# Sixteen 32-byte reads, one for each DMA engine, issued from the Activation queue ahead of the first load of a row-maximum kernel

## The chip, the cores and the metric

One core of a Trainium2 chip. The metric is device time in microseconds (us), median of several executions. A profile's span runs from the first to the last instruction and is about 1.8 us shorter than the device time of the same execution (165.17 and 163.4 us for the profiled run of the kernel before).

## The reference

```python
x = np.random.randn(32, 512, 1024).astype(np.float32)     # 16,384 rows of 4,096 B
return np.max(x, axis=-1).astype(np.float32)
```

## The kernel before

The rows are read in loads of decreasing size into a ring of 45 row slots per partition. Each load has one reduction on VectorE. All loads are issued by SyncE; the two stores at the end are issued by Activation. The first load gives each of 128 partitions 14 rows, which lie in one run of 14 x 4,096 = 57,344 B in memory.

```python
BLOCKS = [
    [14, 13, 12, 11, 9, 8, 8, 7, 6, 5, 5, 4, 4, 3, 3],
    [2, 2, 2, 1, 1, 1, 1, 1, 1, 1, 1, 1],
]
RING = 45
...
    PAD = 16
    tail = once.tile([P, PAD + H], F32)        # columns 0 to 7 are read by nobody
    at = first = 0
    for loads in BLOCKS:
        S = sum(loads) + (loads is BLOCKS[-1])
        xb = xf[first * P:(first + S) * P, :].rearrange("(p i) d -> p i d", p=P)
        ...
        for n in loads:
            if at + n > RING:
                at = 0
            xc = ring[:, at:at + n, :]
            nc.sync.dma_start(out=xc, in_=xb[:, b:b + n, :])
            reduce = nc.vector.reduce_max(out=res[:, first + b:first + b + n], in_=xc, axis=X)
            ...
    ...                                        # last row in two halves, then two stores
```

## Time and profile before

| | kernel before |
|---|---|
| device time | 164.99 us, median of 3 (164.94 to 165.01) |
| DMA queue of the loads | 96.6% of 16 engines' span |
| VectorE | busy 139.0 us, waits for loads 22.1 us, of it 20.31 us for the first |
| first issue, first packet, first reduction | 0.73, 1.72, 20.31 us |

What bounds the kernel, and why an earlier start of the loads should move the end by as much, is worked out in the prediction below. Its words, as this text uses them: an issue is the DMA instruction on the queue of SyncE or Activation; a packet is one record of what one of the 16 DMA engines moved; a load or read has landed when all of its data are there and what waits for it may start. A descriptor is the order for one such piece of work, and the descriptor generator makes the descriptors from an issue. Where an experiment speaks of a queue's ring, the queue's list of descriptors is meant and not the tile `ring`.

A window line can be read for more than its rate. A packet counts, with its whole length, in the stretch in which it starts. So GB/s times the stretch's length, over 57,344 B, is a number of packets; and DMA share times length times 16 is the sum of their durations. For 1.60 to 1.80 us of the kernel before: 1720 GB/s x 0.2 us / 57,344 B = 6 packets, and 5.78 x 0.2 x 16 = 18.5 us, or 3.08 us each. A steady packet takes 2.116 us. What a first packet takes beyond that is called its excess from here on.

### The profile page before, as it was taken

How to read it: one execution, taken by the hardware profiler on the slowest of the kernel's cores; microseconds unless marked ns; L12 is line 12 of the kernel's file. 1: busy time of each engine (PE TensorE's matmuls, PEld its weight loads, DVE VectorE, ACT ScalarE, POOL GpSimd, SP SyncE). 2: the span in 40 equal slices, each digit the busy share in tenths (PEclk: the TensorE clock that was granted, in tenths of full speed). 3: DMA queues.
4: the chain of work that ended last, by engine and by line, in shares of the span. 5: the costliest groups of instructions: out<-in, count | busy, mean ns of one | idle time of the engine just before them, and what ended most of it. 6: DMA issues, size and time to landing. Idle time of an engine off the chain costs nothing.

```text
span 163.4 us, 117 instructions
## 1 busy us (share of the span) xinstructions
DVE 139.0 (85%) x29; POOL 0.2 (0%) x4
## 2 busy tenths in 40 slices
DVE  0000099989998999999999999999999999999994
POOL 0000000000000000000000000000000000000000
DMA  6999999999989989999989999999999999999990
GB/s 225 449 449 449 433 417 417 417 401 529 433 385 430 452 386 432 433 433 441 457 385 481 401 442 422 409 438 421 446 409 425 437 410 422 427 407 409 409 355 16
DMA packets 4464, 67.18 MB, mean 411 GB/s; under 512 B 752, under 2 KB 752, under 8 KB 2160
## 3 DMA queue, kind: packets, MB, share of 16 engines
q1 hardware_dynamic: 4176, 67.11, 96.6%
q10 hardware_dynamic: 288, 0.07, 0.2%
HBM read 67.11 MB, written 0.07 MB: 411 GB/s over the span
## 4 chain that ended last, share of the span: by engine, by line
DVE 49%; DMA 48%; SPq 1%; issue 0%
DMA ring<-in_x_dram 48%; DVE res L58 48%; SPq L57 1%; DVE res L70 0%; DVE tail L69 0%
## 5 line engine op out<-in xcount | busy, mean ns | idle before, releaser
L58 DVE TENSOR_REDUCE res<-ring 128x1 f32<-128x1024 f32 (+12 forms) x27 | 137.7, 5165 | 22.1 <-DMA ring<-in_x_dram 22.1
L70 DVE TENSOR_REDUCE res<-tail 128x1 f32<-128x513 f32 x1 | 0.7, 686 | 0.0
L69 DVE TENSOR_REDUCE tail<-ring 128x1 f32<-128x512 f32 x1 | 0.7, 682 | 0.0
L90 POOL MEMSET const-bfloat16-1.0<- 128x1 bf16 x1 | 0.1, 102 | 0.0
L90 POOL MEMSET const-uint8-127<- 128x1 uint8 x1 | 0.1, 102 | 0.0
L90 POOL MEMSET const-float32-0.0<- 128x1 f32 x1 | 0.1, 99 | 0.2 <-issue 0.2
L90 POOL MEMSET const-float32-1.0<- 128x1 f32 x1 | 0.1, 99 | 0.0
## 6 DMA issues: line engine op xcount, KB each, us to landing
ring<-in_x_dram SPq DMA_DIRECT2D x2, 4096.0 KB, 25.6
ring<-in_x_dram SPq DMA_DIRECT2D x1, 7168.0 KB, 19.6
ring<-in_x_dram SPq DMA_DIRECT2D x1, 6656.0 KB, 34.9
ring<-in_x_dram SPq DMA_DIRECT2D x1, 6144.0 KB, 48.9
ring<-in_x_dram SPq DMA_DIRECT2D x1, 5632.0 KB, 28.5
ring<-in_x_dram SPq DMA_DIRECT2D x2, 2560.0 KB, 38.4
ring<-in_x_dram SPq DMA_DIRECT2D x1, 4608.0 KB, 24.7
ring<-in_x_dram SPq DMA_DIRECT2D x9, 512.0 KB, 13.8
```

The source lines that it names most:

```text
L57: nc.sync.dma_start(out=xc, in_=xb[:, b:b + n, :])
L58: reduce = nc.vector.reduce_max(out=res[:, first + b:first + b + n], in_=xc, axis=X)
L69: nc.vector.reduce_max(out=tail[:, PAD - 1:PAD], in_=half, axis=X)
L70: nc.vector.reduce_max(out=res[:, I - 1:], in_=tail[:, PAD - 1:], axis=X)
L90: nc = _bacc.Bacc("TRN2", target_bir_lowering=False, num_devices=1)
```

## The change

The intent: touch every DMA engine with a tiny read before the first load, so that whatever an engine's first transfer pays is paid by the tiny read. The Activation queue is used so that SyncE's own issue is not held up.

```diff
     PAD = 16
     tail = once.tile([P, PAD + H], F32)
+
+
+    far = xf.rearrange("(q i) d -> q (i d)", q=16)
+    nc.scalar.dma_start(out=tail[:16, :PAD // 2], in_=far[:, :PAD // 2])
 
     at = first = 0
```

## The prediction

> **What bounds the kernel now.** I read four views in this order: the page, the waits, the chain of work that ended last, and then narrow stretches around the first load. The page has only two workers: VectorE (DVE) and the DMA queue that SyncE feeds.
>
> ```profile
> span 163.4 us, 117 instructions
> DVE 139.0 (85%) x29; POOL 0.2 (0%) x4
> q1 hardware_dynamic: 4176, 67.11, 96.6%
> q10 hardware_dynamic: 288, 0.07, 0.2%
> L58 DVE TENSOR_REDUCE res<-ring 128x1 f32<-128x1024 f32 (+12 forms) x27 | 137.7, 5165 | 22.1 <-DMA ring<-in_x_dram 22.1
> ```
>
> The reader is to see that both workers are nearly full. The loads keep 16 DMA engines at 96.6% of the span. DVE is busy 139.0 us and idle 22.1 us, and all of that idle time is a wait for a load. Where the waits lie decides what a change is worth:
>
> ```profile
> 0.73 94.15 SPq L57 DMA_DIRECT2D ring<-in_x_dram  x14
> 20.31 15.09 DVE L58 TENSOR_REDUCE res<-ring 128x14 f32<-128x14336 f32 x1 [20.31 <-DMA ring<-in_x_dram]
> 36.05 14.02 DVE L58 TENSOR_REDUCE res<-ring 128x13 f32<-128x13312 f32 x1 [0.65 <-DMA ring<-in_x_dram]
> 50.58 12.95 DVE L58 TENSOR_REDUCE res<-ring 128x12 f32<-128x12288 f32 x1 [0.51 <-DMA ring<-in_x_dram]
> 63.91 30.14 DVE L58 TENSOR_REDUCE res<-ring 128x11 f32<-128x11264 f32 x3 [0.38 <-DMA ring<-in_x_dram]
> 94.27 8.69 DVE L58 TENSOR_REDUCE res<-ring 128x8 f32<-128x8192 f32 x1 [0.21 <-DMA ring<-in_x_dram]
> ```
>
> Five waits. The last ends at 94.27 us, where the seventh load lands; after it DVE runs to the end without a gap. So the end is the landing of load 7 plus fixed DVE work, and load 7 is one of a row of loads that run back to back from the first byte. **If the first load moves by d and the rate stays, the end moves by d**: loads 1 to 3 are issued at once, and the later ones are released by landings or reductions that move too. So the start matters one for one. There the windows show this (columns: stretch, its length, DVE and GpSimd busy, clock, DMA share, GB/s; a packet counts in the stretch in which it starts):
>
> ```profile
> 1.60:1.80 0.20, 0.00 (x0) 0.00 (x0) 1.00 5.78 1720
> 1.80:2.00 0.20, 0.00 (x0) 0.00 (x0) 1.00 3.68 1147
> 2.00:2.20 0.20, 0.00 (x0) 0.00 (x0) 1.00 1.74 573
> ...
> 2.40:2.60 0.20, 0.00 (x0) 0.00 (x0) 1.00 2.15 860
> 2.60:2.80 0.20, 0.00 (x0) 0.00 (x0) 1.00 0.68 287
> 2.80:4.50 1.70, 0.00 (x0) 0.00 (x0) 1.00 0.00 0
> 4.50:4.70 0.20, 0.00 (x0) 0.00 (x0) 1.00 3.31 1434
> 4.70:4.90 0.20, 0.00 (x0) 0.00 (x0) 1.00 4.63 2007
> 4.90:5.10 0.20, 0.00 (x0) 0.00 (x0) 1.00 1.98 860
> 5.10:5.30 0.20, 0.00 (x0) 0.00 (x0) 1.00 0.66 287
> ```
>
> A packet of the first load is one row of 14 x 4096 = 57,344 B, so 1720 GB/s over 0.2 us is 6 packets, 1147 is 4, and so on: 6 + 4 + 2 + 3 + 1 = 16 first packets, one for each engine, starting between 1.7 and 2.7 us. The second packets (5 + 7 + 3 + 1 = 16) start between 4.5 and 5.3 us. The trace's packet records, read one by one, make it exact: the first packet starts at 1.72 us, second packets start from 4.54 to 5.15 us, and every later packet of this load takes 2.116 us, which is 27.1 GB/s an engine. First packets take up to 3.38 us: **12 of the 16 are 0.5 to 1.26 us longer than a steady one**, and the four shortest (0.00 to 0.06 us over for three of them) are among those that started last. This start-up excess is what the change aims at.
>
> **What the Trainium skill says.** (1) "DMA: Bandwidth & Descriptors", section "Latency and other measured facts": about 600 ns to the first byte on this path, and about 800 ns for the smallest read of HBM. The trace has 0.99 us from the start of the first issue (0.73 us) to the first packet's start (1.72 us), so longer than the page's first figure if the start of a packet stands for its first byte. (2) The same page, "Issuing engines are not separate DMA queues": DMAs of all issuing engines run on the same 16 DMA engines and interleave. So the added reads do reach the engines that the first load uses. (3) The same page, "Why a DMA increments its semaphore by 16 and not by 1": the outer dimension sets how many engines a copy takes; 16 rows give 16, one row each. That fits the change's intent; the kernel before has no copy of this shape to check it with. (4) "Perfetto Trace Analysis", "DMA Instruction — HWDGE (DVE, Sync)": the descriptor generator is locked for one issuer at a time. The trace before has no two issuers at once, so it can't say. No page says anything of a cost of an engine's first use.
>
> **The change, part by part.** It removes nothing. It adds one DMA instruction on the Activation queue, 16 rows of 32 B from places 4 MiB apart, into bytes of the tail tile that nobody reads.
> - Bytes: 512 B against 67.11 MB, nothing.
> - Activation's time: its two stores take 0.38 and 0.34 us to issue, from 159.78 us on. Before that it idles, so a similar third issue at about 0.73 us is free there.
> - Waits: comparing the order of instructions, the eight completion semaphores that DMAs take in turn shift by one place. The only new wait is that the eighth load waits for the 16 small reads, which land some 80 us before it can be issued. Each reduction waits for the same load as before. The last load writes other columns of the tail tile and gets no wait for the reads.
> - Gain: the lead over the first load is small. In the trace SyncE and Activation leave the start barrier 0.005 us apart, so both issue at about 0.73 us. Their race is decided by who generates descriptors faster, 16 against 128 rows. If the cold part is an engine's first access, the reads take it over, but only by as much as they come sooner. I put that lead at 0 to 0.5 us. The ceiling is the slowest engine: its second packet starts at 5.15 us where 1.72 + 2.116 = 3.84 us would be ideal, so 1.3 us.
> - Cost: if the generator is held by Activation when SyncE wants it, the first load starts later by up to one issue, 0.35 us.
> - Sum: a mean gain of about 0.35 us (a quarter of the ceiling) less a mean cost of about 0.15 us (half an issue, taken less than surely), so 0.2 us: 164.99 - 0.2 = 164.8 us.
>
> **The rivals.** *Full gain:* the excess is wholly a first access that a 32 B read can take over, and the reads get there first; the whole row of loads moves by up to 1.3 us, so 163.7 us. For it speaks that steady packets vary by only a few ns, so the excess belongs to the start; against it, that the reads start no earlier than the load, and that the last-starting engines show hardly any excess, as if the delay were one common to all and over at about 2.4 to 2.7 us whatever asked first. *Hidden anyway, or cold elsewhere:* the excess belongs to SyncE's own ring or to the pages that it reads (the added reads touch other addresses), so nothing changes: 165.0 us. *A new wait in its place:* the two issuers queue for the generator and the first load starts late by 0.1 to 0.35 us, and the slowest engine's packets with it: 165.1 to 165.35 us. *DVE as the bound:* it is already the bound from load 7 to the end (94.27 us onward), but this caps nothing, because an earlier start moves load 7 too. At most 22.1 us of waits could ever be taken out and this change reaches only a fraction of the first, 20.31 us.
>
> **Range and chances.** The full gain gives 163.7, the full cost 165.35. I don't give the extremes much weight: 164.2 to 165.25 us should hold it 8 times in 10, with 164.8 us as the prediction. Repeats of the kernel before lie within 164.94 to 165.01 us, so noise adds little. Two per cent would be 3.3 us, more than twice the ceiling of the gain and nine times the cost worked out above. So same has 0.98, faster 0.01, slower 0.01.
>
> **What would show it right or wrong.** In the changed kernel's trace: (a) the packets of the Activation queue should start at or before the first load's; if they come after, the gain is nil. (b) SyncE's first issue should start at 0.73 us and last 0.37 us; a longer or later one is the generator's queue. (c) The 16 second packets should start about 0.2 us earlier at the slowest engine (5.15 us before), and the first reduction at about 20.1 us instead of 20.31. (d) The end should move by the same amount as the first reduction, within 0.1 us, with DVE's busy time at 139.0 us and the wait at load 7 still there. If the first reduction moves and the end doesn't, my chain is wrong, and a later load or the store carries the end. If the end moves more than 1.3 us, the rate of the loads changed, which I hold unlikely since 512 B can't do it.

## The result, and the profile after

The changed kernel took 164.98 us in the median (164.94 to 165.13, 4 runs), the kernel before 164.97 us beside it (164.88 to 165.01, 4 runs). The ratio is 1.0003, with a 95% interval from 0.9986 to 1.0021: the same. Ratios here are the mean time of one kernel's runs over that of the other's of the same rounds, so not quite the ratio of the medians.

The timeline of the changed kernel, with the lines that answer to those of before (start, length, engine, line, operation; L61 and L62 are the old L57 and L58):

```profile
0.72 0.40 ACTq L47 DMA_DIRECT2D tail<-in_x_dram  x1
0.73 94.09 SPq L61 DMA_DIRECT2D ring<-in_x_dram  x14
20.25 15.09 DVE L62 TENSOR_REDUCE res<-ring 128x14 f32<-128x14336 f32 x1 [20.25 <-DMA ring<-in_x_dram]
...
94.19 8.69 DVE L62 TENSOR_REDUCE res<-ring 128x8 f32<-128x8192 f32 x1 [0.21 <-DMA ring<-in_x_dram]
```

Activation issues its reads at the same moment as SyncE its first load (0.725 and 0.730 us). The first reduction starts at 20.25 us instead of 20.31. That 0.06 us must not be credited to the change: this profile is of an execution of 165.00 us, the one of before of an execution of 165.17 us, the slowest of all of that kernel's runs beside it, and the timed runs show no difference. Their interval is wide, though: it reaches from 0.23 us faster to 0.35 us slower, so the times alone can't tell the predicted gain of 0.2 us from none. What the reads did has to be read from the trace.

The windows of the changed kernel over its first packets, and over the second ones:

```profile
1.60:1.80 0.20, 0.00 (x0) 0.00 (x0) 1.00 6.32 2007
1.80:2.00 0.20, 0.00 (x0) 0.00 (x0) 1.00 6.23 2007
2.00:2.20 0.20, 0.00 (x0) 0.00 (x0) 1.00 0.89 287
2.20:2.40 0.20, 0.00 (x0) 0.00 (x0) 1.00 0.88 287
...
4.50:4.70 0.20, 0.00 (x0) 0.00 (x0) 1.00 3.32 1434
4.70:4.90 0.20, 0.00 (x0) 0.00 (x0) 1.00 5.31 2295
4.90:5.10 0.20, 0.00 (x0) 0.00 (x0) 1.00 1.33 574
```

In the first 0.2 us there are 7 packets with 6.32 x 0.2 x 16 / 7 = 2.89 us each: the excess is still there. By the packet records its median is 0.75 us, against 0.76 us before. The other thing to see is what the first four lines lack. A small read would add a packet whose bytes are too few to show; the packet records have none on the Activation queue in this time. Where the reads went is told by the DMA view (size of the issue, then microseconds to landing):

```profile
q10 hardware_dynamic: 320, 0.07, 0.2%
...
tail<-in_x_dram ACTq DMA_DIRECT2D x1, 0.5 KB, 6.8
```

Queue 10 is Activation's; it has 32 packets more than the 288 of before: 16 reads of 32 B and 16 completion writes of 4 B. They took 6.8 us to land. The packet records show why. **On each of the 16 engines the 57,344 B packet came first, and the read stands just behind it**: on the quickest engine, for example, the first packet runs from 1.730 to 4.338 us, the read from 4.335 for 9 ns, the second packet of the load from 4.340 us. The read's completion write waited for that second packet in turn and came at 6.45 us. The Trainium skill, "DMA: Bandwidth & Descriptors", section "Queues, rings and completion order", says that an engine takes turns between queues one whole packet at a time; the trace agrees, with packets of 57,344 B and a wait of 2.6 us.

So the reads warmed nothing, because they ran second. That leaves the more important question: would they have helped, had they run first?

### The profile page after: what moved, and what is told of

It reads as the page before. It is cut to its first block, busy times and chain, and to the rows that moved or that the text cites. A ratio compares the mean times of both kernels' runs of the same rounds, so it can differ in the third digit from the quotient of the medians.

```text
span 163.2 us, 118 instructions
## 1 busy us (share of the span) xinstructions
DVE 138.9 (85%) x29; POOL 0.2 (0%) x4
## 4 chain that ended last, share of the span: by engine, by line
DVE 49%; DMA 48%; SPq 1%; issue 0%
DMA ring<-in_x_dram 48%; DVE res L62 48%; SPq L61 1%; DVE res L74 0%; DVE tail L73 0%
## 5 line engine op out<-in xcount | busy, mean ns | idle before, releaser
L62 DVE TENSOR_REDUCE res<-ring 128x1 f32<-128x1024 f32 (+12 forms) x27 | 137.7, 5162 | 22.0 <-DMA ring<-in_x_dram 22.0
```

## The experiments

Theory A: the excess is a cold first access that a small read can take over, and the change failed only because its reads came late. Theory B: the excess belongs to the opening of a load, whatever went before. Eleven kernels were run. All outputs are right.

**Reads landed before the first load (e1).** The loads wait for the reads (`far` as in the change):

```diff
...
+    warm = nc.scalar.dma_start(out=tail[:16, :PAD // 2], in_=far[:, :PAD // 2])
...
+            load = nc.sync.dma_start(out=xc, in_=xb[:, b:b + n, :])
+            tc.add_manual_dep(load.ins, warm.ins.name, SYNC, reason="the start")
```

> The first load now waits until the 16 small reads have landed, so the reads really come first. Theory A (cold first access that a small read takes over; the change failed only because its reads came behind the first packets): the excess of the first 57,344 B packets over 2.116 us falls from a median of 0.75 us to under 0.1 us; the first load is issued about 2 us later, so the time is about 164.97 + 2.0 - 0.7 = 166.3 us. Theory B (the excess is the ordinary time from a descriptor's start to flowing data, paid by whatever transfer opens an empty queue): the excess stays at 0.6 to 0.9 us and the time is 164.97 plus the whole delay, about 167.0 us.

The DMA view of this run, then its windows over the first packets of the load:

```profile
tail<-in_x_dram ACTq DMA_DIRECT2D x1, 0.5 KB, 2.0
```

```profile
3.60:3.80 0.20, 0.00 (x0) 0.00 (x0) 1.00 6.21 2007
3.80:4.00 0.20, 0.00 (x0) 0.00 (x0) 1.00 4.48 1434
```

Now the reads land in 2.0 us, and the load's first issue starts at 2.71 us. But 6.21 x 0.2 x 16 / 7 = 2.84 us a packet, as before: the excess is 0.68 us in the median, 0.42 us at least. The time was 166.81 us in its one run (state unknown), 1.88 us over the 164.93 us of before in that session, for an issue 1.98 us later (2.71 against 0.73). Theory A expected 166.3, B 167.0; the excess decides for B.

This run also shows how close the race of the change was. Alone, the reads start one after another, 0.047 us apart, from 1.72 to 2.42 us; the first packets of the load in the changed kernel start from 1.72 to 2.29 us. What lets the load win on every engine stays open; e4 below, which issues both in the same way, has the same order on all 16.

**Delay without reads (e2), and a shorter delay, timed (e8).** The control for e1: the loads wait for two VectorE instructions.

```diff
+    idle = once.tile([P, 1024], F32)           # e8: 512
+    nc.vector.memset(idle, 0.0)
+    warm = nc.vector.reduce_max(out=tail[:, 1:2], in_=idle, axis=X)
...
+            tc.add_manual_dep(load.ins, warm.ins.name, SYNC, reason="the start")
```

> Control: no reads, but the first load waits for two VectorE instructions of about 2 us together. Theories A and B both expect the excess of the first packets to stay at 0.6 to 0.9 us in the median and the time to be 164.97 plus the delay of the first issue (about 2 us). If the excess falls here too, mere lapse of time after the launch removes it, and neither reads nor their landing are needed.

> The control of the same rounds: no reads at all, the first load waits for two VectorE instructions of about 1.2 us together. Both theories: time = before + delay of the first issue, within 0.15 us. What e5 gains against this after taking off each one's own delay is all that a perfect warm-up is worth: 0.7 us under theory A, under 0.15 us under theory B.

e2: median excess 0.76 us; 167.66 us in its one run, 2.73 us over before for an issue 2.47 us later, with one engine at 1.31 us of excess setting the pace. e8: median excess 0.62 us; 166.36 us (166.27 to 166.43, 4 runs) against 165.01, so 1.35 us for an issue 1.41 us later. Lapse of time doesn't take the excess away.

**Same queue, same rows, landed first (e5).** As warm as it can be made: 32 B of each of the first load's own rows, on SyncE's queue.

```diff
+    S0 = sum(BLOCKS[0])
+    near = xf[:S0 * P, :].rearrange("(p i) d -> p (i d)", p=P)
+    warm = nc.sync.dma_start(out=tail[:, :PAD // 2], in_=near[:, :PAD // 2])
...
+            tc.add_manual_dep(load.ins, warm.ins.name, SYNC, reason="the start")
```

> As warm as it can be made: 32 B of each of the first load's own 128 rows, read on SyncE's own queue, and the first load waits until they have landed. So ring, engine and addresses have all been used. Theory A in its last form (something cold, but of the ring or the pages and not of the engine): median excess of the first 57,344 B packets under 0.1 us, time = before + delay of the first issue - 0.7 us. Theory B (an opening transfer's ordinary latency or ramp): median excess 0.6 to 0.9 us and time = before + delay, within 0.15 us.

The windows of this run over the first and the second packets of the load:

```profile
3.40:3.60 0.20, 0.00 (x0) 0.00 (x0) 1.00 9.76 3154
3.60:3.80 0.20, 0.00 (x0) 0.00 (x0) 1.00 1.71 573
...
6.20:6.40 0.20, 0.00 (x0) 0.00 (x0) 1.00 5.29 2294
```

Eleven packets start in the first stretch, with 9.76 x 0.2 x 16 / 11 = 2.84 us each; the median excess is 0.66 us. The time was 166.58 us (166.43 to 166.62, 4 runs), 1.57 us over before for an issue 1.74 us later, a net of -0.17 us. The control e8 of the same rounds has a net of -0.06 us. So **a warm-up that has used ring, engine and addresses is worth about 0.11 us by the times**, which is less than the spread of either kernel's four runs (0.19 and 0.16 us) and so not shown to differ from nothing. The traces say the same. The first load's issue and the first reduction, in e5 and then in e8:

```profile
2.47 1.28 SPq L61 DMA_DIRECT2D ring<-in_x_dram  x3
21.84 15.09 DVE L63 TENSOR_REDUCE res<-ring 128x14 f32<-128x14336 f32 x1 [21.84 <-DMA ring<-in_x_dram]
```

```profile
2.14 1.31 SPq L61 DMA_DIRECT2D ring<-in_x_dram  x3
21.51 15.09 DVE L63 TENSOR_REDUCE res<-ring 128x14 f32<-128x14336 f32 x1 [19.40 <-DMA ring<-in_x_dram]
```

From issue to reduction both take 19.37 us, and so does e1 (22.08 - 2.71): warm or not, the load needs the same time. These are single executions; over all runs with this first load it is 19.36 to 19.65 us. In this form the warm-up costs 1.74 us of waiting. Theory A falls in its forms of engine, ring and pages, as far as 32 B reads can warm them. For the pages there is one thing more: the 112 later packets of the first load of the kernel before also read places that nobody had read, and take 2.116 to 2.121 us.

**Reads first on SyncE's queue, without a wait (e3).**

```diff
-    nc.scalar.dma_start(out=tail[:16, :PAD // 2], in_=far[:, :PAD // 2])
+    nc.sync.dma_start(out=tail[:16, :PAD // 2], in_=far[:, :PAD // 2])
```

> The reads are issued by SyncE, ahead of the first load on the same queue, so each engine meets them first without any wait. SyncE's first load is issued one issue later, 0.37 to 0.43 us. Theory A: the reads start 0.4 us ahead and take over that much of the excess, so the first packets' excess falls to about 0.3 us and the time stays within 0.1 us of 164.97. Theory B: the excess stays at 0.6 to 0.9 us and the time rises by the issue, to about 165.4 us.

The reads now start ahead, at 1.71 us, and land in 2.1 us. The load is issued at 1.16 us, 0.43 us later than before, and the time is 165.43 us (4 runs) against 164.93: 0.50 us more, ratio 1.0033 (1.0016 to 1.0049). Eleven of 16 first packets still have over 0.5 us of excess; seven of them start in this window, with 6.31 x 0.2 x 16 / 7 = 2.88 us each:

```profile
2.20:2.40 0.20, 0.00 (x0) 0.00 (x0) 1.00 6.31 2008
```

The reads give nothing back for the issue they cost.

**Second load issued late (e4).** A third theory: the first packets are slow because descriptors of the next two loads are made meanwhile. Here the second load waits for the reads.

```diff
...
+            if first + b == BLOCKS[0][0]:
+                tc.add_manual_dep(load.ins, warm.ins.name, SYNC, reason="the start")
```

> The reads stay where the change has them; the second load is issued only when they have landed, at about 7.6 us, well before the first load is through at 20 us. Theories A and B: nothing changes, excess 0.75 us in the median, time 164.97 within 0.15 us. Theory C (the first packets are slow because the descriptors of loads 2 and 3 are made at the same time): the excess falls below 0.3 us and the time to about 164.5 us.

The second issue moved to 7.44 us, and the median excess stayed at 0.72 us; 164.85 us in one run (state unknown). Not the descriptors.

**A short first load (e6).**

```diff
-    [14, 13, 12, 11, 9, 8, 8, 7, 6, 5, 5, 4, 4, 3, 3],
+    [1, 13, 13, 12, 11, 9, 8, 8, 7, 6, 5, 5, 4, 4, 3, 3],
```

> No reads and no wait; the first load is cut to one row of 4,096 B per partition and the second has 13 rows. If the excess is a latency or ramp in time (theory B), the start up to full rate lasts just as long: the first 53,248 B packets (behind eight of 4,096 B) show what is left of about 0.7 us, and the second packets of that size begin about as late as the bytes allow plus 0.5 to 0.9 us. If the excess belongs to the large size of the first packets, it shrinks with the size and the time falls by about 0.5 us. I expect the former and a time of 164.95 within 0.25 us.

The sixteen 4,096 B packets that start first take 0.20 to 1.01 us; a steady one takes 0.159 us. Two engines do their first packet in about 0.20 us, and each of them shows the delay on its second, with 0.70 and 0.88 us (from 1.926 and 1.930 us): on these the delay is not that of an engine's first access. The 53,248 B packets behind them take 1.966 us from the first on; they start at 3.59 to 4.03 us, where 1.72 + 8 x 0.159 = 2.99 us would be ideal, so 0.60 to 1.04 us late. So the opening costs time, not a share of the first packet's size, and whichever packets come first pay it. The same 14 rows are there at 20.11 us, and the time is 164.87 us in one run (state unknown): no gain. I had expected a rest of the excess on the large packets, and there was none.

**Fewer engines (e7, e9, e10).** If the excess is plain latency (B1), two engines pay it as sixteen do; if it comes of many engines opening together (B2), two don't. The first rows of the load are read by 2 or 8 engines alone, and the loads wait for them.

```diff
...                                            # two: a view of the first load's rows
+    warm = nc.sync.dma_start(out=ring[:2, :14, :], in_=two[:2, :14, :])         # e7
+    warm = nc.sync.dma_start(out=ring[::64, :14, :], in_=two[::64, :14, :])     # e9
+    warm = nc.sync.dma_start(out=ring[:32:4, :14, :], in_=two[:32:4, :14, :])   # e10
```

> Two rows of 57,344 B on two engines alone open the queue, and the real first load waits for them. It tells apart two forms of theory B: if the excess is plain latency, the two packets take about 2.1 + 0.7 us each; if it comes of sixteen engines opening together, the two take 2.12 to 2.3 us, and the sixteen that follow show the excess again. The time is no use here: about 4.5 us more than before.

e7 missed its aim: the two packets went to partitions 0 and 1 and took 4.38 and 4.28 us, about twice 2.116, so they seem to have shared one way into memory. Beyond 2 x 2.116 = 4.232 us they have only 0.15 and 0.05 us. Its time, 171.24 us, is 6.23 us over before instead of the 4.5 expected. The mended runs use partitions further apart:

> The run with two engines, mended: its two packets went to neighbouring partitions and took 4.3 us each, twice 2.12, so they shared a road and the excess could not be read. Here the two rows go to partitions 0 and 64. Plain latency (B1): about 2.8 us each, an excess of 0.6 to 0.9 us. Crowding when 16 engines open together (B2): 2.12 to 2.3 us, an excess under 0.2 us.

> Eight rows on eight engines, partitions 0, 4, ... 28. B1: excess 0.6 to 0.9 us, as with 16. B2: between that of two engines and that of sixteen, 0.2 to 0.5 us in the median. The 16-engine load behind it shows 0.6 to 0.8 us in both.

The issue of e9's two packets and one window line with these two alone, then two more with the 16 of the load behind them; then a line of e10 with its eight:

```profile
0.73 0.63 SPq L47 DMA_DIRECT2D ring<-in_x_dram  x1
...
2.00:2.20 0.20, 0.00 (x0) 0.00 (x0) 1.00 1.44 573
...
5.60:5.80 0.20, 0.00 (x0) 0.00 (x0) 1.00 1.69 573
5.80:6.00 0.20, 0.00 (x0) 0.00 (x0) 1.00 11.53 3727
```

```profile
2.20:4.00 1.80, 0.00 (x0) 0.00 (x0) 1.00 0.72 255
```

Two packets: 1.44 x 0.2 x 16 / 2 = 2.30 us, an excess of 0.19 us. Eight: 0.72 x 1.8 x 16 / 8 = 2.59 us; by the records a median excess of 0.49 us. The sixteen that follow in e9: 11.53 x 0.2 x 16 / 13 = 2.84 us, though the two packets before had ended only some 1.3 us earlier (4.42 and 4.48 us). The least excess among these sixteen is 0.41 us, so the two engines that had just moved 57,344 B each have it again, which speaks against anything cold once more.

| engines opening together | median excess, us |
|---|---|
| 2 (e9) | 0.19 |
| 8 (e10) | 0.49 |
| 16 (before, after, e1, e2, e4, e5, e8, e11) | 0.62 to 0.76 |

That speaks for B2 but doesn't show it. The strided issues of e9 and e10 took 0.63 and 0.77 us instead of 0.37, and their packets start later after the start of the issue (1.39 and 1.51 us instead of 0.99), so part of the smaller excess might be time lost before the record begins. A count that doesn't depend on where a record begins is from the start of the issue to the end of the first packet, less 2.116 us: 1.60 us for two engines, 2.15 for eight, 1.95 for the sixteen of the kernel before (medians). That order is no longer the order of B2. Counted from the end of the issue, the medians are 0.97, 1.39 and 1.58 us, and it is. No run tells which count is right. e7, whose issue took an ordinary 0.34 us, has a small excess too, but with the shared way in it.

**Another pitch (e11).** One row moves from the second block to the first, so that the partitions' first rows stand 452 KiB apart instead of 448 KiB.

```diff
-    [14, 13, 12, 11, 9, 8, 8, 7, 6, 5, 5, 4, 4, 3, 3],
-    [2, 2, 2, 1, 1, 1, 1, 1, 1, 1, 1, 1],
+    [14, 13, 12, 11, 9, 8, 8, 7, 6, 5, 5, 4, 4, 3, 3, 1],
+    [2, 2, 2, 1, 1, 1, 1, 1, 1, 1, 1],
```

> No reads. One row moves from the second block to the first, so the partitions' first rows stand 452 KiB apart in place of 448 KiB. If the opening is slow because all engines start at addresses that differ by a multiple of 64 KiB (B3), the excess falls under 0.3 us and the time by up to 0.5 us. If not (B1, B2), excess 0.6 to 0.8 us in the median and the time 164.98 within 0.25 us (the last small loads stand in a slightly different order, which may cost some tenths).

Median excess 0.64 us, time 165.02 us (4 runs) against 164.99, ratio 1.0001 (0.9984 to 1.0017). A spacing by multiples of 64 KiB is not the cause; other spacings were not tried.

What stays open: whether the excess is plain latency (B1) or crowding (B2), what sixteen engines would contend for in their first 0.7 us, and why the load beat the reads on every engine. No run pointed to a version that beats both kernels: the single runs at 164.85 and 164.87 us (e4, e6) lie within the spread of the kernel before, 164.81 to 165.18 over all sessions.

## Why the prediction was right or wrong

The class and the range were right: 164.98 us lies in 164.2 to 165.25, and within 2% had 0.98. But nothing of the predicted gain of 0.2 us shows, and the reason for a small effect was a different one. That the range held is in part luck: a gain and a cost were put against each other, neither came, and the range had room for nothing at all.

- **What bounds the kernel: held.** Every run in which only the start of the loads moved shows the end moving with it: e3 by 0.50 us for an issue 0.43 us later, e8 by 1.35 for 1.41, e5 by 1.57 for 1.74. All of these moved the start later; no run here moved it earlier.
- **One count was off.** I wrote that 12 of 16 packets were over by 0.5 to 1.26 us; it is 13 (the lowest 0.518), and the other three at most 0.06 us.
- **"Gain", with a lead of 0 to 0.5 us: wrong.** The lead was negative. The reads ran behind the first packets, at 4.34 to 5.09 us on the 16 engines. The prediction's own test (a) named this: if they come after, the gain is nil. The term of 0.35 us was really 0. That 16 rows would be quicker to generate than 128 shows in neither issue: the 16 took 0.401 us (0.381 alone, in e1) and the 128 took 0.372.
- **"Cost", a held descriptor generator, 0.15 us: wrong, 0.** SyncE's issue started at 0.73 us and took 0.372 us with Activation's beside it for all that time, against 0.371 us alone. "Perfetto Trace Analysis", section "DMA Instruction — HWDGE (DVE, Sync)", has a lock; this trace shows no wait for one. Of the sum, -0.35 + 0.15, both terms were 0.
- **The deeper error** stands in the same step: "if the cold part is an engine's first access, the reads take it over". No such part shows in any run: warmed in every way that was tried, the first packets keep 0.66 us of excess (e5), so the ceiling of 1.3 us was not open to such a warm-up. The net worth of one is about 0.11 us by the times, within their spread, and none by the traces.
- **The rivals.** "Hidden anyway, or cold elsewhere" gave the right time, 165.0 us, for a reason that e5 refutes: with the queue's ring used and every row's first bytes read, the excess stays. The remark made against the full gain, that the delay seems common to all engines and soon over, is nearer to the records: in e3 the four packets that start after 2.9 us have 0.25 us of excess or less, and in e6 second packets pay it too.
- **Signs (c) and (d).** The slowest engine's second packet started at 5.10 us instead of 5.15 and the first reduction at 20.25 instead of 20.31, not by 0.2 us, and that difference is one between two executions. VectorE's busy time (138.9 us) and the wait at load 7 (94.19 us) stayed, as foreseen.
- **The wait that the eighth load got** cost nothing: the reads landed at 7.6 us, and VectorE's waits are the same five, 22.0 us in all. The lead was misread: that load is issued at 64.36 us, so the reads land 57 us before, not some 80.

## What to carry to other kernels

Before you warm something up, measure whether the cost is cold at all: let the warm-up land first, whatever that costs, and see if the excess goes; here it didn't, and the trace of the first such run showed it. An instruction that is issued first on another queue need not run first (here it was 0.005 us ahead, and second on all 16 engines): look in the packet records for the order on the engine, and remember that a small read behind a large packet can wait for all of it, here 2.6 us. And subtract each variant's own delay from its time before you compare, with a control that has the delay and not the remedy.

## What the Trainium skill lacked or had wrong

- "DMA: Bandwidth & Descriptors", section "Latency and other measured facts": it has a first-byte time of about 600 ns for this path; here 0.92 to 1.03 us passed from the start of an issue of 0.33 to 0.41 us on SyncE to the first packet's start. From the end of the issue it is 0.58 to 0.63 us, which agrees; the page doesn't say from where it counts. It has no figure for the opening of a large load on this path: when 16 engines open together, a first packet of 57,344 B takes 0.62 to 0.76 us longer than the steady 2.116 us (medians); two engines 0.19 us, behind a longer issue.
- The same page: no word on whether an engine's first use costs anything. These runs show none: about 0.11 us by the times (e5 against e8), which is within the spread of the runs, and 19.37 us from issue to first reduction in both traces.
- The same page, section "Queues, rings and completion order": it gives packets of some 9 to 17 descriptors; the consequence for a small read beside a large load is missing. Here a 32 B read waited behind a packet of 57,344 B, and its completion behind the next one: 6.8 us to landing instead of 2.0.
- "Perfetto Trace Analysis", section "DMA Instruction — HWDGE (DVE, Sync)": it locks the descriptor generator for one issuer; two issues from SyncE and Activation ran side by side from 0.73 us on, in 0.372 and 0.401 us, against 0.371 and 0.381 us alone (before, e1).
- No page has the issue time of a copy to strided partitions: 0.63 us for 2 rows and 0.77 us for 8, against 0.34 us for 2 neighbouring ones.
